# Encoder layer on one core: buffers for z, two later stores of weight sums, and the first token loads requested by ScalarE

## The chip, the cores and the metric

The kernel runs on one core of a Trainium2 chip. The metric is the device time of one execution in microseconds, as a median of several runs.

## The reference

One encoder layer is applied to two sequences of 1024-wide tokens, a prompt of 256 and a sample of 2048. The six parts of the input projection are called q, k, v, z_a, u and z_f here, each 512 wide.

```
h = rms_norm(x, g_pre);  proj = h @ w_in          # q, k, v, z_a, u_f, z_f
y_a = neighbourhood_attention(q, k, v, rpb)       # window of 8 rows x 16 columns on a grid 64 wide
y_f = real(fft2(u_f over tokens and 64 features)) @ w_fourier + b_fourier
mixed = [rms_norm(y_a) * silu(z_a), rms_norm(y_f) * silu(z_f)]
out = x + rms_norm(mixed @ w_out, g_post)
```

All data are float32.

## The kernel before

**Products in three passes.** A float32 product is made from operands split into a rounded part h (written by ScalarE as a cast) and a rest l (written by VectorE as source minus h). `mm3` (L163) then issues three matmuls, h by h, h by l and l by h. So each operand of TensorE costs one ScalarE instruction and one VectorE instruction before it can be used.

**Who orders the work.** From L602 to L971 the order on ScalarE, VectorE, GpSimd and SyncE is the order in which the program's lines run, and TensorE's order is by hand everywhere. Each engine takes its instructions strictly in that order. SyncE issues every DMA of the kernel; a DMA that has to wait for its data or its buffer holds up all those behind it in SyncE's order. Buffers come from pools with tags, and an instruction that takes a buffer waits until the last reader of that buffer, often a store, is through.

**Stage 1 (L623 to L754), first tokens.** v and u are made for six tiles c of 128 tokens, two of the prompt and four of the sample. For the first three tiles the loads come in four parts kp of the contraction, each with two k of v's weights (`RV`) and two of each token tile (`x_part`, L617). `split_w` scales a weight by gpre on ScalarE (L258) and VectorE (L259), `x_split` splits tokens (L288, L289). v's twelve groups come first on TensorE, then u's, whose weights `fold_u` has to form on GpSimd (L269). Before all this TensorE runs idle matmuls (L229), and ScalarE loads its function table and warms it up (L604, L605). `r_sum` forms sums of v's and u's weights, and `r_put` (L456) stores them to `sD`, 1 MB each: five stores, number 0 at L675 and numbers 1 to 4 at L724 to L726, two for c = 3 and two for c = 4. They are read again from L467 on. `iv_get` (L323) loads the reciprocal norms of the sample's tokens spread over all partitions, `n_load` (L389) loads a quarter of transposed sample tokens, 1 MB, `n_scale` (L400) multiplies them by gpre and the reciprocal norm on VectorE, `n_sum` combines them, and `n_first` (L429) splits one of the results: a ScalarE cast of 128 by 2048 (L432) and a VectorE subtraction of the same size (L433).

**Stage 2 (L757 to L792), the prompt's other products.** Sixteen blocks b of z_f, z_a, k and q for the 256 prompt tokens, each with 24 matmuls of 256 columns. `wz_load` (L698) loads the weights of one block, 512 KB; `b_raw` (L562) splits them (L566 and L567, or L569 and L570 for q). It works two blocks ahead: block b carries `b_raw(b + 2)`, then one of `n_scale` (two instructions), `n_sum` or nothing, then perhaps `n_first` or `op_split`. At the end of each block ScalarE evacuates the product (L788) into a buffer of the tag f, of which there are 3, and SyncE stores it (L790, L792). The results of stage 1 leave through the same three buffers (`vu_out`, L335).

**Stage 3 (L819 to L848) and stage 4 (L834 to L969).** v and u of the rest, and then z_f, z_a, k and q of the sample, are made by a scheme with fewer products: sixteen rounds i with seven products j, from sums of weights (`w_sums`, L534, split in `a_split`, L545) and sums of tokens. Within a round VectorE adds products up in tiles of the tag e (6 buffers of 512 floats; `e_`, L853: u0, u2, u4, u3) and writes two outputs o of 1024 floats each, in the tag f (3 buffers), which are stored at j = 5 and j = 6 (L878, L880).

**The Fourier stage inside rounds 8 to 15.** For 16 values n2, `u_load` (L364) fetches a slice of u, `u_split` (L369) splits it (ScalarE L371, VectorE L372), and `u_stage1` (L374) multiplies it by a 128-point transform (`pz`), copies the result z out of the accumulator on ScalarE (L379) and stores it to `ZD` (L380). Each round takes three of them, at j = 1, 3 and 5. z has the tag f, whose other two buffers hold the round's outputs. ScalarE's copy of z stands in order before its casts for the next weights (L550) and for the next slice (L371).

**After L971** the four DMA and vector engines are ordered by a planner; the change touches nothing there.

Of the kernel before, what the change touches and what calls it, by code (L numbers as in the profile page):

```python
# [10 lines left out]
F32 = mybir.dt.float32  # L11
# [151 lines left out]
def mm3(nc, out, lh, ll, rh, rl, first, last):  # L163
    nc.tensor.matmul(out, lh, rh, start=first, stop=False)  # L164
    nc.tensor.matmul(out, lh, rl, start=False, stop=False)  # L165
    nc.tensor.matmul(out, ll, rh, start=False, stop=last)  # L166


def build(tc, A, O):
    nc = tc.nc  # L170
# [24 lines left out]
    ones = cst.tile([128, 1], F32, name="ones")  # L195
# [17 lines left out]
    st = ph.enter_context(tc.tile_pool(name="st", bufs=2))  # L213
# [17 lines left out]
    def gt(shape, dtype, name):  # L231
        return gp.tile(shape, dtype, tag="g", name=name)

    def load(shape, src, name):
        t = gt(shape, F32, name)
        nc.sync.dma_start(t, src)
        return t
# [7 lines left out]
    def k8(dtype, name, shape=(128, 4, 512)):  # L245
        return hp.tile(list(shape), dtype, tag="k8", name=name, bufs=NK)
# [27 lines left out]
    def xsrc(c):  # L274
        return A["xt"][c] if c < 2 else A["xs"][c - 2]
# [47 lines left out]
    def iv_get(c0, n):  # L323
        t = ivb[c0] = hp.tile([128, 1024], F32, tag="vw", name="iv", bufs=3)
        nc.sync.dma_start(t[:, :128 * n],
                          ivD[c0:c0 + n].rearrange("(o c) p -> o (c p)", o=1).to_broadcast([128, 128 * n]))
# [47 lines left out]
    def u_stage1(n2):  # L374
        t = uu_.pop(n2)
        pz = ps.tile([128, 512], F32, tag="b", name="pz", bufs=2)
        mm3(nc, pz, f1h, f1l, t[:, 0], t[:, 1], True, True)
        z = st.tile([128, 512], F32, tag="f", name="z", bufs=3)
        nc.scalar.copy(z, pz)  # L379
        nc.sync.dma_start(ZD[:, n2, :], z)  # L380

# [7 lines left out]
    def n_load(x):  # L389
        if type(x) is tuple:  # L390
            nq[x] = k8(F32, "nx")
            nc.sync.dma_start(nq[x], A["xq"][0, x[0], x[1]])
            return
        nx = [k8(F32, "nx") for kh in range(2)]
        for kh in range(2):
            for b in range(2):
                nq[x, kh, b] = nx[kh][:, 2 * b:2 * b + 2]
                nc.sync.dma_start(nq[x, kh, b], A["xq"][1, kh, b][:, 2 * x:2 * x + 2])

    def n_scale(x, kh, b, ks=range(4)):  # L400
        v_ = nq[kh, b] if x is None else nq[x, kh, b]
        for k in ks if x is None else range(2):
            kk = 4 * kh + 2 * (x or 0) + k
            nc.vector.scalar_tensor_tensor(out=v_[:, k], in0=v_[:, k], scalar=gpre[:, kk:kk + 1],
                                           in1=ivb[2 if x is None else 10][:, 512 * b:512 * b + 512], op0=ALU.mult, op1=ALU.mult)
# [23 lines left out]
    def n_first(j):  # L429
        src = nq[((0, 0), (1, 0), (0, 0), (0, 1), "t3", (1, 0), (1, 1))[j]]  # L430
        h, l = bnew[0, j] = [k8(F32R, "x" + x) for x in "hl"]
        nc.scalar.copy(h, src)  # L432
        nc.vector.tensor_tensor(out=l, in0=src, in1=f_(h), op=ALU.subtract)  # L433
# [22 lines left out]
    def r_put(x):  # L456
        nc.sync.dma_start(sD[x], (RU[1], RV[0], RU[0], RU[1], RV[1])[x])
# [26 lines left out]
    def et(name):  # L484
        return st.tile([128, 512], F32, tag="e", name=name, bufs=6)
# [76 lines left out]
    def b_raw(b):  # L562
        wh, wl = [gt(BS, F32R, "w" + x) for x in "hl"]
        src = wp_[b]
        if b < 12:
            nc.scalar.copy(wh, src)  # L566
            nc.vector.tensor_tensor(out=wl, in0=src, in1=wh.bitcast(F32), op=ALU.subtract)  # L567
        else:
            nc.scalar.activation(wh, src, AF.Copy, scale=-0.125)  # L569
            nc.vector.scalar_tensor_tensor(out=wl, in0=src, scalar=-0.125, in1=wh.bitcast(F32), op0=ALU.mult,  # L570
                                           op1=ALU.subtract)
        wb[b] = wh, wl
# [28 lines left out]
    man = ExitStack()  # L601
    man.enter_context(tc.manual_schedule(engines=MAN))  # L602
    warm = cst.tile([128, 1], F32, name="warm")
    nc.scalar.preload_act_table_set("natural_log_exp_and_others")  # L604
    nc.scalar.copy(warm, ones)  # L605
    f1 = st.tile([128, 128], F32, name="f1", bufs=1)
    f1h = st.tile([128, 128], F32R, name="f1h", bufs=1)
    f1l = st.tile([128, 128], F32R, name="f1l", bufs=1)
# [1 line left out]
    acc, xs, xh, xm = {}, {}, {}, {}  # L610
# [6 lines left out]
    def x_part(c, kp):  # L617
        if kp == 0:
            xs[c] = gt(BS, F32, "xr")
        ks = slice(2 * kp, 2 * kp + 2)  # L620
        nc.sync.dma_start(xs[c][:, ks], xsrc(c)[:, ks])

    nc.sync.dma_start(RV[0][:, 0], A["wv"][0][:, 0])  # L623
    nc.sync.dma_start(gpre, A["gpre"])
# [1 line left out]
    x_part(1, 0)  # L626
    nc.sync.dma_start(RV[0][:, 1], A["wv"][0][:, 1])
    x_part(2, 0)
    for kp in range(4):
        ks = slice(2 * kp, 2 * kp + 2)  # L630
        v = part(RV[kp // 2], kp)
        if kp:
            nc.sync.dma_start(v, part(A["wv"][kp // 2], kp))
            for c in range(3):
                x_part(c, kp)
        split_w("v", v[:, 0:1], (0,))
        x_split(0, ks)
        if kp == 0:
            x_split(1, ks)
        split_w("v", v[:, 1:2], (0,))  # L640
        if kp:
            x_split(1, ks)
        x_split(2, ks)
# [54 lines left out]
    def wz_load(n):  # L698
        for x in range(n):
            wp_.append(load(BS, A["wz"][len(wp_)], "wr"))  # L700
# [17 lines left out]
    for c in range(3, 6):  # L718
        if c == 3:
            iv_get(0, 2)  # L720
        if c < 5:
            wz_load(3)
            x_split(c + 1)
        if c < 5:  # L724
            for x in range(2 * c - 5, 2 * c - 3):
                r_put(x)  # L726
        if c == 4:
            n_load((0, 0))
            iv_get(2, 8)
            xp = k8(F32, "xp", (128, KC, 256))  # L730
            hp_, lp_ = [k8(F32R, "p" + x, (128, KC, 256)) for x in "hl"]
            for k in range(KC):
                for t in range(2):
                    ts = slice(128 * t, 128 * t + 128)
                    nc.vector.scalar_tensor_tensor(out=xp[:, k, ts], in0=xs[t][:, k], scalar=gpre[:, k:k + 1],
                                                   in1=ivb[0][:, ts], op0=ALU.mult, op1=ALU.mult)
            nc.scalar.copy(hp_, xp)
            nc.vector.tensor_tensor(out=lp_, in0=xp, in1=f_(hp_), op=ALU.subtract)
        if c == 5:
            n_load((1, 0))  # L740
            b_raw(0)
            b_raw(1)
        p_mm("v", c, range(4))
        vu_out("v", c)
        if c == 5:
            for b in range(2, 4):
                b_raw(b)
                n_scale(None, 0, 0, range(2 * b - 4, 2 * b - 2))
        p_mm("u", c, range(4))
        if c == 3:  # L750
            iv_rows(2, 8)
        vu_out("u", c)
        if c == 3:
            iv_put(2, 8)  # L754


    for b in range(16):  # L757
        kind, blk = divmod(b, 4)
        if b < 10:
            wz_load(1)  # L760
        if b in (0, 2):
            n_load((b // 2, 1))
        if b == 10:
            op_load(0)
        if b == 12:
            op_load(1)
        if 2 <= b < 14:
            b_raw(b + 2)
        if 2 <= b < 8:
            x, y = divmod(b, 2)  # L770
            n_scale(None, *divmod(x, 2)[::-1], range(2 * y, 2 * y + 2))
        elif 8 <= b < 12:
            n_sum(b - 8)
        if b in (3, 5, 12, 13):
            n_first((3, 5, 12, 13).index(b))
        if b > 13:
            op_split(b - 14)
        p = mmt(512)[:, :TP]
        wh, wl = wb.pop(b)
        for k in range(KC):  # L780
            mm3(nc, p, wh[:, k], wl[:, k], hp_[:, k], lp_[:, k], k == 0, k == KC - 1)
        o = st.tile([128, 256], F32, tag="f", name="f", bufs=3)
        if kind % 2:
            i, d = p, o
        else:
            i = p.rearrange("p (b r c) -> p b r c", b=2, c=32)
            d = o.rearrange("p (r b c) -> p b r c", b=2, c=32)
        nc.scalar.activation(d, i, AF.Silu if kind < 2 else AF.Copy)  # L788
        if kind < 2:
            nc.sync.dma_start(zD[kind, blk * 128:blk * 128 + 128, :TP], o)  # L790
        else:
            nc.sync.dma_start((kD if kind == 2 else qD)[blk, :, :TP], o)  # L792
# [41 lines left out]
    for i in range(16):  # L834
# [48 lines left out]
        for j in range(7):  # L883
# [29 lines left out]
            if sg == 0:  # L913
                x, y = divmod(7 * (pr - 1) + j, 14)
# [17 lines left out]
            for f, d in ((u_load, 0), (u_split, 4), (u_stage1, 6)):  # L932
                x = 7 * pr + j - 7 - d
# [43 lines left out]
    kp = es.enter_context(tc.tile_pool(name="kp", bufs=2, side="right"))  # L977
# [569 lines left out]
    for k in range(2, len(G) + 1):  # L1547
        pr, i = divmod(k, 9)
        g, f = G[k] if k < len(G) else None, G[k - 1] if k else None
# [19 lines left out]
        x = k // 2 + 1  # L1569
# [63 lines left out]
        if 32 <= k < 36:  # L1633
            x, d = k - 32, atiles[k - 32]
# [122 lines left out]
```

## Time and profile before

| what | value |
|---|---|
| median of 3 runs | 982.48 us (980.37 to 988.38) |
| the profiled execution | 981.93 us, span 980.1 us |
| TensorE busy | 963.9 us (98%) |
| VectorE, ScalarE, GpSimd busy | 705.7, 497.3, 431.0 us |
| granted TensorE clock | 0.999 |
| DMA, mean over the span | 286 GB/s |

In the profile's rows PE is TensorE, DVE VectorE, ACT ScalarE, POOL GpSimd and SPq the DMA issues of SyncE. A row of the timeline gives start, duration, engine, line, operation, output and input, how many were merged, and in brackets the idle time ahead of it and what ended that. A row of groups gives busy time and mean nanoseconds, then the idle time ahead of the group. A row of windows gives the length of the stretch, the busy time and count of each engine, the granted clock, the share of the DMA engines and the GB/s. Matmuls overlap, so the pace of TensorE is the distance from start to start.

### The profile page before, as it was taken

The page shows a single profiled execution, that of the slowest core. Times are in us where ns is not written, and L with a number is a line of the kernel's source. Part 1 is how long each engine was busy: PE and PEld are TensorE (multiplying, and loading weights), DVE is VectorE, ACT ScalarE, POOL GpSimd, SP SyncE. Part 2 cuts the span into 40 slices and gives each one's busy share as a digit, 9 for nine tenths or more (in the row PEclk, how much of TensorE's full clock was granted, in tenths as well). Part 3 has the DMA queues.
Part 4 walks back from the last instruction along what each step waited for, and adds up shares of the span by engine and source line. Part 5 has one row for each costly group of instructions (what it writes and reads, how often), then busy time and mean ns, then how long its engine had stood idle before and what let it go on. Part 6 is the DMA issues. An engine that isn't in the chain of part 4 may idle for free.

```text
span 980.1 us, 17001 instructions
## 1 busy us (share of the span) xinstructions
PE 963.9 (98%) x5761; PEld 804.7 (82%) x5761; DVE 705.7 (72%) x1301; ACT 497.3 (51%) x1068; POOL 431.0 (44%) x400
## 2 busy tenths in 40 slices
PE   9999999999999999999999999999999999999996
PEld 7889988888888888887887879888888888888885
DVE  5747988687886877796776445776666666659997
ACT  5836676423335533333334255677666676654443
POOL 3200002455752202755664033477587686534544
PEclk9999999999999999999999999999999999999999
DMA  8899586557759996598887998598787998979993
GB/s 311 321 375 375 195 319 247 196 197 275 275 200 361 360 411 231 214 368 287 316 310 266 332 334 324 184 297 277 243 239 233 290 317 260 294 250 335 332 347 123
DMA packets 146450, 279.89 MB, mean 286 GB/s; under 512 B 13162, under 2 KB 84284, under 8 KB 142972
## 3 DMA queue, kind: packets, MB, share of 16 engines
q1 hardware_dynamic: 146364, 278.80, 81.7%
q8 instruction: 46, 0.75, 0.3%
q14 instruction: 40, 0.33, 0.1%
HBM read 184.37 MB, written 101.72 MB: 292 GB/s over the span
## 4 chain that ended last, share of the span: by engine, by line
PE 52%; DVE 1%; DMA 1%; issue 1%; POOL 1%; ACT 0%; DVEq 0%; SPq 0%; POOLq 0%; ACTq 0%
PE po L1427 20%; PE pv L1497 5%; PE ptb L1481 5%; PE s L1176 4%; PE mm L166 3%; PE mm L165 3%; PE mm L164 3%; PE pab L1019 2%; DMA ZD<-z 1%; PE py L164 1%; PE py L166 1%; PE py L165 1%; PE pz L165 0%; DVE ut L372 0%; PE ppq L1057 0%
## 5 line engine op out<-in xcount | busy, mean ns | idle before, releaser
L164 PE MATMUL mm<-xh,wa 128*128 128x512 f32 x448 | 174.4, 389 | 0.0
L166 PE MATMUL mm<-xh,wa 128*128 128x512 f32 x448 | 174.4, 389 | 0.0
L165 PE MATMUL mm<-xl,wa 128*128 128x512 f32 x448 | 174.4, 389 | 0.0
L536 POOL TENSOR_TENSOR ws<-wr 128x512 f32<-128x512 f32 x16 | 23.2, 1449 | 229.7 <-DMA wr<-wz 217.6
L1210 POOL TENSOR_SCALAR w<-w,m 128x480 f32<-128x480 f32 (+6 forms) x136 | 85.9, 644 | 43.7 <-DVE m L1207 38.5
L165 PEld LDWEIGHTS mm<-xl,wa 128*128 128x128 f32 x448 | 84.1, 188 | 17.6
L164 PEld LDWEIGHTS mm<-xh,wa 128*128 128x128 f32 x448 | 84.1, 188 | 17.6
L166 PEld LDWEIGHTS mm<-xh,wa 128*128 128x128 f32 x448 | 84.1, 188 | 17.4
L1427 PE MATMUL po<-wo,yh 128*128 128x512 f32 x272 | 90.5, 413 | 0.0
L551 DVE TENSOR_TENSOR wa<-wr,wa 128x512 fp32r<-128x512 f32 x60 | 67.0, 1125 | 32.2 <-ACT wa L550 32.1
L1203 ACT ACTIVATE w<-w,m 128x480 f32<-128x480 f32 (+6 forms) x136 | 79.2, 585 | 15.4 <-DVE m L1198 15.4
L1427 PE MATMUL po<-w,yh 128*128 128x512 f32 x280 | 86.7, 391 | 0.0
L1198 DVE CUSTOM_DVE_ANT_1 w<-s,tb 128x360 f32<-128x360 f32 (+5 forms) x124 | 62.5, 541 | 8.4 <-PE s L1176 7.6
L589 POOL TENSOR_TENSOR mt<-mt,rmask 128x880 f32<-128x880 f32 (+2 forms) x24 | 51.6, 2165 | 38.3 <-DVE mt L585 30.2
L165 PE MATMUL mm<-vl,xh 128*128 128x512 f32 x168 | 65.5, 390 | 0.2 <-DVE vl L482 0.2
L164 PE MATMUL mm<-vh,xh 128*128 128x512 f32 x168 | 65.4, 389 | 0.0
L166 PE MATMUL mm<-vh,xl 128*128 128x512 f32 x168 | 65.4, 389 | 0.0
L872 DVE TENSOR_TENSOR f<-u,mm 128x512 f32<-128x512 f32 x64 | 43.5, 680 | 26.0 <-PE mm L166 21.0
L1427 PEld LDWEIGHTS po<-w,yh 128*128 128x128 f32 x280 | 52.3, 188 | 10.8 <-issue 0.2
L1481 PE MATMUL ptb<-ident,w 128*120 128x128 f32 (+5 forms) x428 | 59.6, 277 | 0.1
L1497 PEld LDWEIGHTS pv<-pt,v 120*64 120x64 f32 (+6 forms) x896 | 48.2, 136 | 12.9 <-issue 11.4
L1485 DVE COPY pt<-ptb 120x384 f32<-120x384 f32 (+6 forms) x72 | 41.0, 569 | 24.6 <-PE ptb L1481 24.0
(253 smaller groups left out, 2391.8 us busy)
## 6 DMA issues: line engine op xcount, KB each, us to landing
wr<-wz SPq DMA_DIRECT2D x48, 512.0 KB
vl<-sD SPq DMA_DIRECT2D x20, 512.0 KB
xm<-xm SPq DMA_DIRECT2D x9, 1024.0 KB
oD<-ofs SPq DMA_DIRECT2D x18, 512.0 KB
of<-oD SPq DMA_DIRECT2D x18, 512.0 KB
yr<-yD SPq DMA_DIRECT2D x34, 256.0 KB
zD<-f SPq DMA_DIRECT2D x16, 512.0 KB
woD<-wo SPq DMA_DIRECT2D x16, 512.0 KB
```

The source lines that it names most:

```text
L164: nc.tensor.matmul(out, lh, rh, start=first, stop=False)
L165: nc.tensor.matmul(out, lh, rl, start=False, stop=False)
L166: nc.tensor.matmul(out, ll, rh, start=False, stop=last)
L551: nc.vector.tensor_tensor(out=o[:, 1], in0=src, in1=o[:, 0].bitcast(F32), op=ALU.subtract)
L589: nc.gpsimd.tensor_tensor(out=o, in0=i, in1=rmask[:, m0:m0 + n].unsqueeze(2).to_broadcast([128, n, 80]), op=ALU.add)
L872: nc.vector.tensor_tensor(out=dst(f, b), in0=src(uu[u]), in1=src(p), op=op)
L1198: nc.vector.tensor_tensor_reduce(out=rows(g["w"][b][:, h, :n], w), in0=rows(g["s"][2 * b + h][:, :n], w), in1=tv, scale=1.0, scalar=3.0e38 ...
L1203: nc.scalar.activation(w, w, AF.Exp, bias=m[:, h:h + 1], scale=-1.0, accum_out=m[:, 2 + h:3 + h])
L1210: nc.gpsimd.tensor_scalar(w, w, m[:, 4 + h:5 + h], 1.0, ALU.mult, ALU.mult)
L1427: nc.tensor.matmul(p, (d["l"] if x == 2 else d["h"])[:, c], w(n, int(x == 1), c), start=j == 0, stop=j == 11)
L1481: nc.tensor.transpose(ptb[h][:nk, j * 128:j * 128 + 128], g["w"][b][:, h, c0:c0 + nk], ident)
L1497: nc.tensor.matmul(p[hs, b], g["v"][:nk, v, hs], g["pt"][b][:nk, h, j * 128:j * 128 + 128], start=j == 0, stop=j == len(ch) - 1)
```

## The change

z takes a buffer of the tag e in place of the tag f. The first parts (kp = 0) of the three token tiles are requested by ScalarE in place of SyncE, and ScalarE's table load and warm-up stand behind these requests. Of the stores of weight sums, number 1 stays at c = 3, number 2 goes to c = 4 behind `n_load((0, 0))` and `iv_get(2, 8)`, and numbers 3 and 4 go into blocks 5 and 7 of the prompt's products. At c = 5, the two `b_raw` stand ahead of the four `n_scale`, and behind them `n_first(0)`, which was in block 3; the weight load of block 0 and `n_load((0, 1))` come there too, ahead of the store of u for c = 5.

```
-        z = st.tile([128, 512], F32, tag="f", name="z", bufs=3)
+        z = et("z")
         nc.scalar.copy(z, pz)
         nc.sync.dma_start(ZD[:, n2, :], z)
...
-    nc.scalar.preload_act_table_set("natural_log_exp_and_others")
-    nc.scalar.copy(warm, ones)
...
-        nc.sync.dma_start(xs[c][:, ks], xsrc(c)[:, ks])
+        (nc.sync if kp else nc.scalar).dma_start(xs[c][:, ks], xsrc(c)[:, ks])
...
     x_part(2, 0)
+    nc.scalar.preload_act_table_set("natural_log_exp_and_others")
+    nc.scalar.copy(warm, ones)
...
-        if c < 5:
-            for x in range(2 * c - 5, 2 * c - 3):
-                r_put(x)
+        if c == 3:
+            r_put(1)
         if c == 4:
             n_load((0, 0))
             iv_get(2, 8)
+            r_put(2)
...
         if c == 5:
-            for b in range(2, 4):
-                b_raw(b)
-                n_scale(None, 0, 0, range(2 * b - 4, 2 * b - 2))
+            b_raw(2)
+            b_raw(3)
+            wz_load(1)
+            n_load((0, 1))
+            n_scale(None, 0, 0)
+            n_first(0)
...
-        if b < 10:
+        if 1 <= b < 10:
             wz_load(1)
-        if b in (0, 2):
-            n_load((b // 2, 1))
+        if b == 2:
+            n_load((1, 1))
+        if b in (5, 7):
+            r_put(b // 2 + 1)
...
-        if b in (3, 5, 12, 13):
-            n_first((3, 5, 12, 13).index(b))
+        if b in (5, 12, 13):
+            n_first((5, 12, 13).index(b) + 1)
```

## Prediction

> **What bounds the kernel now.** I read the engine shares first, then the waits of TensorE, then every distance from start to start of its matmuls in stages 1 to 4.
>
> ```profile
> PE 963.9 (98%) x5761; PEld 804.7 (82%) x5761; DVE 705.7 (72%) x1301; ACT 497.3 (51%) x1068; POOL 431.0 (44%) x400
> ```
> ```profile
> PE pz L165 <- DVE ut L372: 3.6, 3, 2.0
> PE mm L166 <- DVE wl L567: 2.0, 2, 1.1
> ```
>
> TensorE is the bound, and no edit removes a matmul. The change can only win back time in which TensorE stands or runs slowly. That is 980.1 - 963.9 = 16 us over the whole span, and the two longest waits above lie where the change works. Three places matter: the Fourier slices, the prompt's blocks, and the first microseconds.
>
> **z in the sums' buffers.** The first row of the next fence is the group of z copies in the rounds 8 to 15; then come two of them, the store ahead of the first, and what TensorE did.
>
> ```profile
> L379 ACT COPY z<-pz 128x512 f32<-128x512 f32 x16 | 9.4, 587 | 48.6 <-DMA ZD<-z 34.9 <-PE pz L166 8.6 <-DVE u L950 3.6
> ```
> ```profile
> 440.84 0.33 SPq L380 DMA_DIRECT2D ZD<-z  x1
> ```
> ```profile
> 450.52 0.59 ACT L379 COPY z<-pz 128x512 f32<-128x512 f32 x1 [8.47 <-DMA ZD<-z]
> ...
> 516.42 0.59 ACT L379 COPY z<-pz 128x512 f32<-128x512 f32 x1 [8.73 <-DMA ZD<-z]
> ```
> ```profile
> 455.13 0.50 PE L165 MATMUL pz<-ut,f1h 128*128 128x512 f32 x1 [1.95 <-DVE ut L372]
> 455.47 0.40 PE L166 MATMUL pz<-ut,f1l 128*128 128x512 f32 x1
> 455.70 0.39 PE L164 MATMUL mm<-xh,wa 128*128 128x512 f32 x1
> ...
> 519.04 0.51 PE L164 MATMUL pz<-ut,f1h 128*128 128x512 f32 x1 [0.45 <-ACT ut L371]
> 520.97 0.50 PE L165 MATMUL pz<-ut,f1h 128*128 128x512 f32 x1 [1.42 <-DVE ut L372]
> ```
>
> The two outputs hold two of the three f buffers, so each z waits for the store of the z before it: issued at 440.84, it frees the copy at 450.52, 9.7 us later. In that time ScalarE cannot make the casts queued behind the copy, for the next weights and the next slice. VectorE's subtractions follow late, and TensorE waits 1.95 us at 455.13 and 0.45 + 1.42 us behind the copy of 516.42. That is 3.82 us. The first matmuls after a wait also come slower, 0.34 us apart (455.13 to 455.47) against 0.23 (455.47 to 455.70). The five slow starts at these places add some 0.7 us. Lost in all: 4.5 us. With three or more free e buffers no z waits for a store, the casts run on time, and all 4.5 us come back. Removing the other waits in the 34.9 us is worth nothing, because TensorE did not stand there. The slice's loads and the round's stores behind z on SyncE's queue only move earlier. What now waits for z's store is a sum of the next round. A round asks for seven e buffers (four sums, three z) out of six, so a buffer comes round again after six requests, nearly a whole round. A round takes 7 products of 12 matmuls and three slices of 3, 93 matmuls at 0.227 us or 21 us, against a store of 9.7 us. Ends: 4.5 us gained, and a loss if reuse comes at once (the third rival). I take 4.5.
>
> **The prompt's blocks.** Rows of TensorE, then groups of VectorE in 83 to 123.3 us, then windows.
>
> ```profile
> 73.06 0.28 PE L164 MATMUL mm<-ph,wh 128*128 128x256 f32 x1
> 73.18 0.28 PE L165 MATMUL mm<-pl,wh 128*128 128x256 f32 x1
> ...
> 91.67 0.39 PE L166 MATMUL mm<-ph,wl 128*128 128x256 f32 x1 [0.94 <-DVE wl L567]
> ...
> 98.79 0.39 PE L166 MATMUL mm<-ph,wl 128*128 128x256 f32 x1 [1.10 <-DVE wl L567]
> ...
> 123.14 0.39 PE L164 MATMUL mm<-vh,xh 128*128 128x512 f32 x1
> ```
> ```profile
> L567 DVE TENSOR_TENSOR wl<-wr,wh 128x1024 fp32r<-128x1024 f32 x8 | 9.8, 1222 | 2.3 <-ACT wh L566 2.3
> L433 DVE TENSOR_TENSOR xl<-nx,xh 128x2048 fp32r<-128x2048 f32 x4 | 9.2, 2289 | 0.0
> ```
> ```profile
> 58.00:78.00 20.00, 20.00 (x110) 17.39 (x109) 7.42 (x9) 8.02 (x9) 0.00 (x0) 1.00 1.02 415
> 83.00:100.00 17.00, 14.96 (x123) 14.55 (x122) 16.73 (x18) 11.66 (x15) 0.00 (x0) 1.00 1.00 396
> 100.00:123.30 23.30, 22.69 (x184) 21.96 (x182) 23.30 (x17) 14.68 (x18) 0.00 (x0) 1.00 0.54 177
> ```
>
> 384 matmuls at 0.12 us would take 46.1 us. They take 123.14 - 73.06 = 50.1 us, so 4.0 us are lost, and another 0.5 us at the first product behind them, where the start after next is again late. VectorE is the cause: busy in all of 83 to 123.3 us but for 2.3 us at its beginning. From 83.27 on the stage ends when VectorE's list ends. `n_first(0)` takes its subtraction, 2.29 us (2.2 net of overlap), out of that list and puts it where VectorE is busy 7.42 us of 20. Its ScalarE cast goes the same way, and the two subtractions and four scalings of c = 5 only change order. So the list ends 2.2 us sooner.
>
> What may undo it is how the list begins:
>
> ```profile
> 77.73 0.69 ACT L339 ACTIVATE uo<-mm,invt 128x512 f32<-128x512 f32 x1 [3.42 <-DMA vN<-vo]
> ...
> 82.19 1.04 ACT L566 CAST wh<-wr 128x1024 fp32r<-128x1024 f32 x1
> ```
> ```profile
> 73.09 1.23 DVE L567 TENSOR_TENSOR wl<-wr,wh 128x1024 fp32r<-128x1024 f32 x1 [5.38 <-issue]
> 77.09 1.42 DVE L404 SCALAR_TENSOR_TENSOR nx<-nx,gpre,iv 128x512 f32<-128x512 f32 x2 [2.77 <-DMA iv<-ivD]
> ...
> 83.27 1.23 DVE L567 TENSOR_TENSOR wl<-wr,wh 128x1024 fp32r<-128x1024 f32 x1 [2.30 <-ACT wh L566]
> ```
> ```profile
> 60.59 0.33 SPq L457 DMA_DIRECT2D sD<-ru  x1
> 63.04 0.33 SPq L457 DMA_DIRECT2D sD<-rv  x1
> ...
> 64.22 0.32 SPq L325 DMA_DIRECT2D iv<-ivD  x1
> ```
>
> ScalarE's cast for block 4 comes at 82.19, in order behind the evacuation of u at 77.73, which waited for a store. The reciprocal norms, requested at 64.22, land at 77.09, 12.9 us later, with the DMA engines full (1.02, 415 GB/s). The stores at 60.59 and 63.04 and number 2 no longer stand ahead of them: 3 MB less, some 7 us at 415 GB/s, so they land near 70 us. The scalings then follow the two splits: 73.09 plus 2 x 1.2 plus 2 x 1.42 us (each row holds two) is 78.3. The cast of `n_first(0)`, twice the size of the one of 1.04 us at 82.19, ends near 80.3 and its subtraction near 82.6. ScalarE evacuates u only behind the cast, near 80 instead of 77.73. The f buffers it needs after that wait for stores that now have 3 MB less ahead of them, so I expect the cast for block 4 within 0.5 us of 82.2. If the buffer that holds the split back to 73.09 comes sooner, all of this is 2 to 3 us earlier, and the whole 4.5 us could return. `wz_load` and `n_load((0, 1))` at c = 5 are issued in the time in which SyncE waits for u's evacuation anyway. The two stores in blocks 5 and 7 cost 2 x 1 MB at 396 GB/s, 2.6 us each, ahead of weight loads and of the stores that free the f buffers. Weights are used four blocks (11.5 us) after their request, and after 100 us the DMA engines are half idle (0.54). Ends: 0 and 4.5 us gained. I take 2.2, the one subtraction.
>
> **The first microseconds.**
>
> ```profile
> 0.73 1.28 ACT L604 ACT_TABLE_LOAD   x1 [0.73 <-PEq L1748]
> 2.03 0.19 ACT L605 COPY warm<-ones 128x1 f32<-128x1 f32 x1
> 4.17 0.72 ACT L258 ACTIVATE wc<-rv,gpre 128x512 fp32r<-128x512 f32 x1 [1.95 <-DMA gpre<-gpre]
> ...
> 9.77 0.72 ACT L258 ACTIVATE wc<-rv,gpre 128x512 fp32r<-128x512 f32 x1 [2.54 <-DMA rv<-wv]
> ```
> ```profile
> 1.64 0.91 SPq L621 DMA_DIRECT2D xr<-xt  x2
> ```
> ```profile
> 10.84 0.49 PE L164 MATMUL mm<-wc,xh 128*128 128x512 f32 x1 [0.39 <-ACT xh L288]
> ```
> ```profile
> 2.00:9.00 7.00, 6.71 (x30) 5.27 (x30) 2.51 (x5) 2.73 (x7) 0.00 (x0) 1.00 0.82 238
> ```
> ```profile
> 5.24 0.50 PE L164 MATMUL mm<-wc,xh 128*128 128x512 f32 x1
> ...
> 23.80 0.39 PE L164 MATMUL mm<-wc,xh 128*128 128x512 f32 x1
> ```
>
> v's 72 matmuls for three tiles run from 5.24 to 23.80, 18.6 us against 72 x 0.227 = 16.3, so 2.2 us are lost. Two token requests cost SyncE 0.91 us, three cost 1.4 us. Without them every later request goes out up to 1.4 us sooner, among them v's weights that ScalarE got at 9.77. ScalarE starts with three requests, 1.4 us by SyncE's rate, then 1.28 + 0.19 us: done near 3.6, while gpre lands at 4.17. So the moved table load costs nothing; without that cover of 0.6 us it would cost what goes beyond it, and at twice SyncE's rate per request that is 0.8 us. The DMA engines were 0.82 busy in 2 to 9 us, so 1.26 us of transfer time can be filled. Ends: 0.8 lost and 2.2 gained; I take half of the 1.26, or 0.7 gained.
>
> By the Trainium skill, "DMA: Bandwidth & Descriptors", section "Issuing engines are not separate DMA queues", requests from two engines share the same 16 DMA engines and save only the time of issuing; the share of 0.82 above leaves room for that saving, and by the rule alone at full DMA engines the term would be 0 (976 to 975 in the sum). By its page "ScalarE: Activation LUTs", section "What ACT_TABLE_LOAD costs", 1.38 us of drain follow a load of 1.28 us, which would make ScalarE late by some 0.8 us; here the warm-up at 2.03 directly follows a load that ends at 2.01, so the trace does not bear it out.
>
> **The sum.** 981.93 - 4.5 - 2.2 - 0.7 = 974.5 us. The profiled execution is 0.55 us under the median of the three runs, 982.48, so it stands for them.
>
> **The rivals.**
>
> All stalls go: the chain of stores eases so much that the prompt's blocks run at 0.12 us throughout. For it speaks that iv, u's evacuation and the f buffers all wait for one full DMA queue; against it, that VectorE needs about 3.3 us a block from block 8 on (a split of 1.2 and `n_sum` or `n_first` of 2.29, less overlaps) against 2.88 on TensorE. 981.93 - 4.5 - 4.5 - 2.2 = 970.7.
>
> The prompt's gain is given back: ScalarE's cast of `n_first(0)` pushes u's evacuation and all behind it, or the two stores delay the f buffers, so that VectorE's list starts or stands 2.2 us later. For it speaks that the cast at 82.19 has only 1.1 us to spare; against it, the 3 MB. 981.93 - 4.5 - 0.7 = 976.7.
>
> The z stores hold up the sums, the slower side: if a sum is given the buffer of the last z at once, it waits up to 9.7 us per round for the store, on ScalarE or VectorE. In the rounds VectorE is free for 116 - 80.2 us (row below), about 6.5 us a round; what exceeds that, 3.2 us in six rounds, adds 19 us, and 2.9 us are gained elsewhere: 998. It decides only once the buffer is asked for less than 9.7 us after the store, and the rotation of six speaks against that.
>
> ```profile
> 430.00:546.00 116.00, 111.98 (x489) 91.30 (x489) 80.19 (x94) 45.11 (x77) 62.24 (x35) 1.00 0.87 309
> ```
>
> The change does not do what it says for z: the slices wait for their own loads or for VectorE instead, and the 4.5 us stay. 981.93 - 2.9 = 979.0.
>
> **How the numbers follow.** Forecast 974.5 (within 1.5 us): 0.45. All stalls go: 0.13. Prompt's gain lost: 0.21. z's gain replaced: 0.14. z holds the sums: 0.04. Something else slower: 0.03. From 970.0 to 980.5 lie the first four and their noise, 0.85 or so. A measurement of this kernel can tell about 1%, 9.8 us; only the first rival, and it in part, goes beyond that: faster 0.11, same 0.84, slower 0.05.
>
> **What would show it.** Right: no z copy waits for ZD; no TensorE wait near 455 and 520; the last prompt block ends 2 us sooner after its first; the subtraction of `n_first(0)` lies before 83 us; ScalarE's first weight still starts near 4.2. Wrong: waits of sums for ZD; the cast for block 4 later than 84; the waits at blocks 6 and 8 unchanged; v's first 72 matmuls not shorter.

## The result and the profile after

The changed kernel takes 972.22 us (median of 8 runs, 971.13 to 973.84), the kernel before beside it 981.42 us (8 runs, 978.64 to 988.38). The ratio is 0.990, with a 95% interval of 0.9874 to 0.9926: 9.2 us less, against a forecast of 974.5 and about as much as the 1% that the prediction called the limit of what can be told. The profiled execution after took 971.13 us, with a span of 969.3 us against 980.1; its granted clock is 0.997, before 0.999, so the clock did not give the gain.

From the page of the changed kernel, the engine shares; below it all that is left of TensorE's waits (engine, line, what was waited for: us in all, times, longest).

```profile
PE 960.3 (99%) x5761; PEld 805.3 (83%) x5761; DVE 709.3 (73%) x1301; ACT 496.7 (51%) x1068; POOL 430.2 (44%) x400
```
```profile
PE idle L229 <- POOL onesq L225: 1.0, 1, 1.0
PE mm L164 <- ACT xh L288: 0.9, 1, 0.9
PE mm L165 <- DVE vl L482: 0.2, 1, 0.2
```

The waits for `ut` and for `wl`, 3.6 and 2.0 us before, are gone. To see where the time came from, the prediction's landmarks are looked up again. TensorE's timeline after:

```profile
6.29 0.50 PE L164 MATMUL mm<-wc,xh 128*128 128x512 f32 x1 [0.87 <-ACT xh L288]
...
23.14 0.39 PE L164 MATMUL mm<-wc,xh 128*128 128x512 f32 x1
...
72.40 0.28 PE L164 MATMUL mm<-ph,wh 128*128 128x256 f32 x1
...
118.69 0.39 PE L164 MATMUL mm<-vh,xh 128*128 128x512 f32 x1
```

| TensorE, start in us | before | after | gained in this stretch |
|---|---|---|---|
| first product of u | 23.80 | 23.14 | 0.66 |
| first product of the prompt's blocks | 73.06 | 72.40 | 0.00 |
| first product behind the blocks | 123.14 | 118.69 | 3.79 |
| first Fourier slice (`pz`) | 431.18 | 426.73 | 0.00 |
| last Fourier slice | 542.42 | 532.61 | 5.36 |

These are 9.81 of the span's 10.8 us. The remaining 1.0 us lies in the stages after, which the change does not touch. All thirteen kernels of this document have the same code there and take 436.7 to 438.5 us for it, so it is not claimed for the change.

**The slices.** The group of z copies on ScalarE in 420 to 536 us (busy us, mean ns, then the idle time ahead of it), then TensorE's group of the products behind `ut`, and the window:

```profile
L379 ACT COPY z<-pz 128x512 f32<-128x512 f32 x16 | 9.4, 589 | 27.6 <-PE pz L166 23.0 <-issue 4.5
```
```profile
L165 PE MATMUL pz<-ut,f1h 128*128 128x512 f32 x16 | 6.2, 389 | 0.0
```
```profile
420.00:536.00 116.00, 116.00 (x513) 96.05 (x512) 85.00 (x99) 45.70 (x78) 67.60 (x37) 1.00 0.92 329
```

Before, 34.9 of 48.6 us of ScalarE's idle time ahead of z ended with a store of z. Those were 5 of the 16 copies. Now no such wait is left: z waits for its own product (the 4.5 us of "issue" are one copy, at 524.24, right behind the last matmul of its product at 523.77), and TensorE is busy in all of the 116 us.

**The prompt's blocks.** First VectorE, then ScalarE, then SyncE's issues, in the changed kernel:

```profile
68.82 2.54 DVE L567 TENSOR_TENSOR wl<-wr,wh 128x1024 fp32r<-128x1024 f32 x2 [3.03 <-ACT wh L566]
71.28 2.73 DVE L404 SCALAR_TENSOR_TENSOR nx<-nx,gpre,iv 128x512 f32<-128x512 f32 x4
75.98 2.29 DVE L433 TENSOR_TENSOR xl<-nx,xh 128x2048 fp32r<-128x2048 f32 x1 [1.97 <-ACT xh L432]
79.76 1.23 DVE L567 TENSOR_TENSOR wl<-wr,wh 128x1024 fp32r<-128x1024 f32 x1 [1.48 <-ACT wh L566]
```
```profile
74.05 1.90 ACT L432 CAST xh<-nx 128x2048 fp32r<-128x2048 f32 x1 [4.31 <-DVE nx L404]
75.86 0.68 ACT L339 ACTIVATE uo<-mm,invt 128x512 f32<-128x512 f32 x1
...
78.69 1.04 ACT L566 CAST wh<-wr 128x1024 fp32r<-128x1024 f32 x1
```
```profile
59.07 0.33 SPq L325 DMA_DIRECT2D iv<-ivD  x1
...
88.31 0.47 SPq L457 DMA_DIRECT2D sD<-ru  x1
...
94.03 0.46 SPq L457 DMA_DIRECT2D sD<-rv  x1
```
```profile
83.00:100.00 17.00, 17.00 (x144) 17.00 (x144) 16.34 (x18) 9.64 (x13) 0.00 (x0) 1.00 1.02 395
100.00:118.70 18.70, 18.70 (x157) 18.54 (x155) 18.70 (x12) 13.25 (x16) 0.00 (x0) 1.00 0.65 233
```

The reciprocal norms are requested 5 us sooner than before (59.07 against 64.22), and the scalings follow the splits without a wait. The subtraction of `n_first(0)` begins at 75.98. VectorE's list for block 4 starts at 79.76, 7.36 us behind the first product of the blocks, against 83.27 and 10.21 before. VectorE is still busy in nearly all of 83 to 118.7 us, and the two stores fall into a time of full DMA engines (1.02), but TensorE no longer waits: the blocks take 46.29 us, and 384 times 0.12 is 46.1.

**The first microseconds.** ScalarE in the changed kernel (ACTq are its DMA issues):

```profile
0.74 0.89 ACTq L619 DMA_DIRECT2D xr<-xt  x2
1.66 0.45 ACTq L619 DMA_DIRECT2D xr<-xs  x1
2.14 1.28 ACT L627 ACT_TABLE_LOAD   x1 [2.14 <-issue]
3.43 0.19 ACT L628 COPY warm<-ones 128x1 f32<-128x1 f32 x1
5.22 0.72 ACT L258 ACTIVATE wc<-rv,gpre 128x512 fp32r<-128x512 f32 x1 [1.60 <-DMA gpre<-gpre]
...
7.94 0.73 ACT L258 ACTIVATE wc<-rv,gpre 128x512 fp32r<-128x512 f32 x1 [0.29 <-DMA rv<-wv]
```

The first weight starts at 5.22, not near 4.2: gpre comes 1.05 us later. The second part of v's weights is split at 7.94 in place of 9.77. In this profile 0.66 us are left of it at u's first product.

### The profile page after: what moved, and what is told of

The parts are those of the page before. It is cut to its first block, busy times and chain, and to the rows that moved or that the text cites. A ratio compares the mean times of both kernels' runs of the same rounds, so it can differ in the third digit from the quotient of the medians.

```text
span 969.3 us, 17001 instructions
## 1 busy us (share of the span) xinstructions
PE 960.3 (99%) x5761; PEld 805.3 (83%) x5761; DVE 709.3 (73%) x1301; ACT 496.7 (51%) x1068; POOL 430.2 (44%) x400
## 4 chain that ended last, share of the span: by engine, by line
PE 97%; DVE 1%; POOL 1%; issue 0%; DMA 0%; ACT 0%; DVEq 0%; SPq 0%; POOLq 0%; ACTq 0%
PE po L1432 20%; PE mm L165 18%; PE mm L166 18%; PE mm L164 18%; PE pv L1502 5%; PE ptb L1486 5%; PE s L1181 4%; PE pab L1024 2%; PE py L164 1%; PE py L166 1%; PE py L165 1%; DMA gpre<-gpre 0%; PE ppq L1062 0%; PE pz L166 0%; PE pz L165 0%
## 5 line engine op out<-in xcount | busy, mean ns | idle before, releaser
L1432 PEld LDWEIGHTS po<-w,yh 128*128 128x128 f32 x280 | 52.3, 188 | 10.8 <-issue 0.2
L550 ACT CAST wa<-wr 128x512 fp32r<-128x512 f32 x60 | 36.4, 617 | 45.1 <-PE mm L166 18.8
```

The lines of the kernel that those rows point to most:

```text
L1432: nc.tensor.matmul(p, (d["l"] if x == 2 else d["h"])[:, c], w(n, int(x == 1), c), start=j == 0, stop=j == 11)
```

## The experiments

**Each part of the change alone or undone**, four kernels beside the kernel before (980.93 us).

`z_only` is the kernel before with one line changed.

```
-        z = st.tile([128, 512], F32, tag="f", name="z", bufs=3)
+        z = et("z")
```

> The kernel before with z in the sums' buffers and nothing else. If z's waits for its own store are what held TensorE in rounds 8 to 15, the stretch from the first to the last pz matmul shrinks from 111.2 us to about 105.9 (as in the changed kernel, 532.61 - 426.73), everything ahead of it stays, and the time is 5.4 us under the kernel before. If instead that stretch became dense because the rounds start 4.5 us sooner against the DMA queue, at least 2 us of the waits stay and the gain is 3 us or less.

Measured: 976.1 us, ratio 0.9951 (0.9936 to 0.9965). The first to the last slice take 431.44 to 537.29, 105.85 us against 111.24 before: 5.4 us, where nothing earlier has changed. ScalarE's group in 420 to 536 us (the sixteenth copy lies behind the window):

```profile
L379 ACT COPY z<-pz 128x512 f32<-128x512 f32 x15 | 8.8, 588 | 27.6 <-PE pz L166 23.0 <-issue 4.5
```

So the slices' gain comes from this line alone, and it is the same with the other edits as without them (105.88 and 105.85 us).

`stores_back` is the changed kernel with the weight sums' stores 1 to 4 back at c = 3 and c = 4.

```
-        if c == 3:
-            r_put(1)
+        if c < 5:
+            for x in range(2 * c - 5, 2 * c - 3):
+                r_put(x)
...
-            r_put(2)
...
-        if b in (5, 7):
-            r_put(b // 2 + 1)
```

> The changed kernel with the stores 1 to 4 of weight sums back at c = 3 and c = 4. Theory A (one subtraction less in VectorE's list gives 2.2 us, the lighter DMA queue the other 1.6): the prompt's blocks take 47.8 us from first to last matmul instead of 46.2, the time is 1.6 us above the changed kernel. Theory B (the lighter DMA queue gives all, since the list starts 3.5 us sooner by it): the norms land near 76 again, the cast of n_first(0) stands ahead of u's evacuation and pushes the cast for block 4 to 83 or later, the blocks take 49.5 us or more, 3.5 us or more above the changed kernel.

`first_back` is the changed kernel with `n_first(0)` back in block 3.

```
-            n_first(0)
...
-        if b in (5, 12, 13):
-            n_first((5, 12, 13).index(b) + 1)
+        if b in (3, 5, 12, 13):
+            n_first((3, 5, 12, 13).index(b))
```

> The changed kernel with n_first(0) back in block 3. Theory A: VectorE's list is 2.2 us longer, the blocks take 48.4 us, 2.2 us above the changed kernel. Theory B: the list starts 1 to 2 us sooner still, since u's evacuation no longer stands behind the cast, and the blocks stay within 1 us of 46.2.

Measured: 976.74 us (ratio 0.9953, 0.9939 to 0.9968) and 975.49 us (0.9948, 0.9929 to 0.9966). These medians may not be the price of the edit alone. Each of the two profiles has a wait of 1.2 to 1.3 us near 350 us, in a stage that the edit does not touch; three other kernels have 0.3 us there and the rest none, and whether the edits bring it about is not shown. In the profile with the stores back the first matmuls also ran at half pace (below), which puts u's first product at 24.62 us, 1.5 us later. So the blocks are read by themselves, from their own first product on. VectorE with the stores back, then ScalarE's cast for block 4 there, then VectorE with `n_first(0)` back:

```profile
73.92 2.48 DVE L567 TENSOR_TENSOR wl<-wr,wh 128x1024 fp32r<-128x1024 f32 x2 [6.57 <-issue]
76.66 2.74 DVE L404 SCALAR_TENSOR_TENSOR nx<-nx,gpre,iv 128x512 f32<-128x512 f32 x4 [0.26 <-DMA iv<-ivD]
81.36 2.29 DVE L433 TENSOR_TENSOR xl<-nx,xh 128x2048 fp32r<-128x2048 f32 x1 [1.97 <-ACT xh L432]
84.86 1.23 DVE L567 TENSOR_TENSOR wl<-wr,wh 128x1024 fp32r<-128x1024 f32 x1 [1.20 <-ACT wh L566]
```
```profile
83.78 1.05 ACT L566 CAST wh<-wr 128x1024 fp32r<-128x1024 f32 x1
```
```profile
79.94 1.23 DVE L567 TENSOR_TENSOR wl<-wr,wh 128x1024 fp32r<-128x1024 f32 x1 [5.74 <-ACT wh L566]
...
85.30 2.28 DVE L433 TENSOR_TENSOR xl<-nx,xh 128x2048 fp32r<-128x2048 f32 x1
```

| | blocks, us | VectorE's list begins, us after the first block |
|---|---|---|
| before | 50.08 | 10.21 |
| stores back | 48.6 | 10.97 |
| `n_first(0)` back | 47.65 | 7.35 |
| changed kernel | 46.29 | 7.36 |

With the stores back the blocks are 2.3 us longer, with `n_first(0)` back 1.4 us. Together they are 3.7 of the 3.8 us of the change. With the stores back the row at 73.92 starts behind 6.57 us in which VectorE waited for nothing that the profile names; with them moved it starts at 68.82 (69.01 with `n_first(0)` back). With `n_first(0)` back the list begins just as soon, but it is one subtraction of 2.28 us longer. Neither the theory that the subtraction alone does it nor the one that the stores alone do it holds: the list starts sooner because the stores were moved, and it is shorter because of `n_first(0)`.

**What held the split.** The row at 73.92 names only "issue". The rows beside it tell more. With the stores back, these are TensorE's last two matmuls for u, which read the two halves xh and xl of c = 5's tokens, and ScalarE's next cast:

```profile
73.44 0.39 PE L165 MATMUL mm<-wc,xh 128*128 128x512 f32 x1
73.66 0.39 PE L166 MATMUL mm<-wc,xl 128*128 128x512 f32 x1
```
```profile
74.09 1.05 ACT L566 CAST wh<-wr 128x1024 fp32r<-128x1024 f32 x1 [3.81 <-PE mm L166]
```

The last read of xh ends at 73.83, and VectorE begins the split's subtraction at 73.92; the last read of xl ends at 74.05, and ScalarE begins the cast at 74.09. The programs built from the kernels agree: in the kernel before, `z_only` and `stores_back`, these two writes are given the very buffers of xh and xl of c = 5 (13 buffers of one tag hold tokens and weights), and VectorE's has to wait for TensorE. In the changed kernel and in `first_back` they are given the buffers of the raw weights of blocks 0 and 1, whose splits end at 65.8 us in the changed kernel. So no store held the split. Moving the stores in the program changed which buffer the split gets when the program is built.

The stores also act while the kernel runs: with them back, the scalings behind the split still wait 0.26 us for the norms, until 76.66, so another buffer for the split would by itself hardly have let them begin sooner. In the changed kernel they begin at 71.28 and wait for neither. No run has the one without the other.

`gpre_first` is the changed kernel with gpre requested ahead of v's first weights.

```
+    nc.sync.dma_start(gpre, A["gpre"])
     nc.sync.dma_start(RV[0][:, 0], A["wv"][0][:, 0])
-    nc.sync.dma_start(gpre, A["gpre"])
```

> The changed kernel with gpre requested ahead of v's first weights on SyncE. If gpre came late in the changed kernel (5.22 instead of 4.17) because it stood behind 256 KB on its own queue, ScalarE's first weight comes near 4.2 again and the first product near 5.3 instead of 6.29, u's first product 0.5 to 1 us sooner. If it came late because the three token loads share the DMA engines with v's first weights, those weights become what ScalarE waits for, and the first product stays within 0.3 us of 6.29.

Measured: 975.01 us, 0.9940 (0.9919 to 0.9961), worse than both expectations. ScalarE's first weight, TensorE's first product, and the window of 8 to 10 us:

```profile
6.68 0.72 ACT L258 ACTIVATE wc<-rv,gpre 128x512 fp32r<-128x512 f32 x1 [3.05 <-DMA rv<-wv]
```
```profile
7.74 0.50 PE L164 MATMUL mm<-wc,xh 128*128 128x512 f32 x1 [2.49 <-ACT xh L288]
```
```profile
8.00:10.00 2.00, 2.00 (x5) 1.54 (x5) 2.00 (x6) 1.98 (x5) 0.00 (x0) 0.53 0.90 237
```

Now v's weights come last, later than gpre did, and behind the gap of 2.49 us TensorE was granted half the clock (0.53): u's first product is at 26.02. When gpre itself landed cannot be seen here. The order of these two requests only changes which of the two ScalarE waits for last.

**Who requests the first tokens**, in two more groups (the kernel before 982.67 and 983.56 us). `sync_requests` is the changed kernel with SyncE requesting the first parts again, `two_requests` the one in which ScalarE requests two of the three, `one_request` the one in which it requests the third alone, behind its table load in the program.

```
# sync_requests
+        nc.sync.dma_start(xs[c][:, ks], xsrc(c)[:, ks])
# two_requests
+        (nc.sync if kp or c == 2 else nc.scalar).dma_start(xs[c][:, ks], xsrc(c)[:, ks])
# one_request, x_part(2, 0) behind the warm-up
+        (nc.scalar if kp == 0 and c == 2 else nc.sync).dma_start(xs[c][:, ks], xsrc(c)[:, ks])
# each in place of
-        (nc.sync if kp else nc.scalar).dma_start(xs[c][:, ks], xsrc(c)[:, ks])
```

> The changed kernel with the first three token loads requested by SyncE again (the table load still behind where they stood). If these requests gave 0.7 us, ScalarE's first weight comes at 4.2 instead of 5.2, the first product at 5.25, but u's first product 0.6 to 0.9 us later than the 23.14 of the changed kernel, and the time is 0.7 us above it. If the loads were bound by the DMA engines and not by SyncE's issue time, u's first product comes within 0.2 us of 23.14 and the time is the same.

> The changed kernel with only the two prompt tiles requested by ScalarE; the sample's tile goes to SyncE behind v's second weight. If gpre lands late because 384 KB of tokens share the DMA engines with 256 KB of v's weights, a third of the tokens less brings ScalarE's first weight from 5.2 to about 4.8 and the first product to 5.9, and u's first product 0.2 to 0.4 us sooner. If the request itself on a second queue delays gpre, the first weight stays at 5.2.

> The changed kernel with the two prompt tiles requested by SyncE as before and only the sample's tile by ScalarE, behind its table load. If the early requests on a second queue are what delays gpre, the first weight is back at 4.2 and the first product at 5.25, v's later weights come about 0.45 us sooner than with all requests on SyncE, u's first product comes at 23.2 to 23.5, and no gap is left in which the clock could fall. The time is that of the changed kernel within 0.5 us.

ScalarE's first weight in each, in that order:

```profile
4.18 0.72 ACT L258 ACTIVATE wc<-rv,gpre 128x512 fp32r<-128x512 f32 x1 [1.96 <-DMA gpre<-gpre]
```
```profile
5.92 0.72 ACT L258 ACTIVATE wc<-rv,gpre 128x512 fp32r<-128x512 f32 x1 [2.79 <-DMA gpre<-gpre]
```
```profile
5.21 0.72 ACT L258 ACTIVATE wc<-rv,gpre 128x512 fp32r<-128x512 f32 x1 [2.99 <-DMA gpre<-gpre]
```

| | first weight | first product | u's first product | median us | ratio to before |
|---|---|---|---|---|---|
| SyncE requests all | 4.18 | 5.25 | 23.69 | 972.04 | 0.9899 (0.9877 to 0.9922) |
| ScalarE one | 5.21 | 6.27 | 24.46 | 973.11 | 0.9899 (0.9863 to 0.9934) |
| ScalarE two | 5.92 | 6.99 | 25.39 | 973.15 | 0.9907 (0.9889 to 0.9926) |
| ScalarE three (changed kernel) | 5.22 | 6.29 | 23.14 | 972.22 | 0.9900 (0.9874 to 0.9926) |

The runs of one and two requests came out later than expected: a single early request of ScalarE is enough to delay gpre by 1 us, and the bytes that ScalarE asks for don't order the delays (two requests, in one profile, are worse than three, which gave 5.22 to 5.55 in seven kernels). In both, the first matmuls also ran at half pace. `one_request` did not hold its request back as meant: it went out at 0.91 us, since only its place among ScalarE's rows was moved and ScalarE does not wait for its table load there. Without any such request gpre is back at 4.18, and u comes 0.55 us later than in the changed kernel; of that nothing is seen in the medians.

**The gap ahead of the first product.** `idle_13` runs 13 idle matmuls first in place of 10, `idle_5` five.

```
-    for x in range(10):
+    for x in range(13):     # idle_13;  range(5): idle_5
```

> The changed kernel with 13 idle matmuls of TensorE at its start instead of 10 (same result). In the changed kernel the first product comes 0.9 us after the idle ones end, and in two of the other runs the products behind such a gap of 0.9 and 2.5 us came 0.42 us apart instead of 0.23. Theory: TensorE left idle loses its clock; three more idle matmuls, 1.2 us by the 0.4 us of one, close the gap, the first product stays within 0.4 us of 6.3, the products behind it come 0.23 us apart in this run, and the median is up to 0.7 us below the changed kernel. Rival: the slow products have another cause (their operands come late one by one) and come as before in some runs; the median does not move.

> The changed kernel with 5 idle matmuls of TensorE at its start instead of 10 (same result), so that some 3 us lie between the idle ones and the first product. If such a gap costs TensorE its clock, the granted clock falls to about 0.5 for some 3 to 4 us behind the first product, its products come 0.42 us apart, and u's first product comes 1.3 to 2 us later than the 23.14 of the changed kernel. If the slow pace has another cause, the clock stays at 1.00 and u's first product within 0.4 us of 23.3.

Measured: 972.86 us, 0.9904 (0.9885 to 0.9923), for 13, and 974.01 us (one run) for 5. With 13 the gap only shrinks to 0.69 us and u's first product comes at 23.30: the expected gain over 23.14 is not seen, and 972.86 lies within the spread of the changed kernel. With 5 the gap is 3.01 us, and matmuls that were 0.23 us apart are 0.43 us apart:

```profile
6.51 0.80 PE L164 MATMUL mm<-wc,xh 128*128 128x512 f32 x1 [3.01 <-ACT xh L288]
...
8.02 0.63 PE L164 MATMUL mm<-wc,xh 128*128 128x512 f32 x1
8.45 0.63 PE L165 MATMUL mm<-wc,xh 128*128 128x512 f32 x1
```

They stay so until about 10.1 us, and u's first product is at 24.69, 1.55 us later. So half the pace for 3.5 us came as expected; the granted clock, expected near 0.5, stayed at 1.00 in every window of these us. `idle_5` has fewer idle matmuls as well as the longer gap, but `gpre_first`, with all ten and a gap of 2.49 us, came to the same pace. The changed kernel's profile has a gap of 0.87 us and the full pace behind it. That is not a rule for such gaps: `stores_back`, with the same start and 0.85 us, has the half pace.

**How many buffers z needs.** `z_own_one` gives z one buffer of its own; the sums keep theirs to themselves.

```
-        z = et("z")
+        z = st.tile([128, 512], F32, tag="zo", name="z", bufs=1)
```

> The changed kernel with one buffer of z's own instead of the sums' six; the outputs keep all three of theirs. If z's number of buffers is what counts, this is what z had before: z waits for its own last store, up to 9 us, the pz stretch grows from 105.9 to 110 us or more, and the time is 4 to 5.5 us above the changed kernel. If the gain was the outputs' third buffer, the stretch stays at 106 and the time is the same.

Measured: 978.56 us, 0.9954 (0.9935 to 0.9974); the slices take 427.04 to 540.95, 113.9 us, more than before the change. ScalarE's group of z copies, then TensorE:

```profile
L379 ACT COPY z<-pz 128x512 f32<-128x512 f32 x16 | 9.4, 587 | 56.4 <-DMA ZD<-z 54.9 <-issue 1.5
```
```profile
516.00 0.50 PE L164 MATMUL pz<-ut,f1h 128*128 128x512 f32 x1 [1.53 <-ACT ut L371]
517.93 0.68 PE L165 MATMUL pz<-ut,f1h 128*128 128x512 f32 x1 [1.42 <-DVE ut L372]
518.41 0.63 PE L166 MATMUL pz<-ut,f1l 128*128 128x512 f32 x1
```
```profile
518.00:520.00 2.00, 2.00 (x5) 1.62 (x6) 0.47 (x1) 1.49 (x3) 0.00 (x0) 0.52 0.91 311
```

The wait for z's store is back on ScalarE, ahead of 10 of the 16 copies where it was 5 before the change, and with it the same kind of waits of TensorE for `ut`. This shows the mechanism from the other side: what counts is that a store of z need not end before the next copy. It also shows that such waits can cost the clock: 0.52 granted behind two of them.

**The two loads at c = 5.** `loads_back` puts the weight load of block 0 and `n_load((0, 1))` back into block 0.

```
-            wz_load(1)
-            n_load((0, 1))
...
-        if 1 <= b < 10:
+        if b < 10:
...
-        if b == 2:
-            n_load((1, 1))
+        if b in (0, 2):
+            n_load((b // 2, 1))
```

> The changed kernel with the weight load of block 0 and n_load((0, 1)) back in blocks 0. If they only fill time in which SyncE waits anyway, the prompt's blocks still take 46.2 us and the time is that of the changed kernel. If their place ahead of u's store matters, VectorE's list starts 1 us or more later or sooner than 7.4 us behind the first block, and with a later start the blocks take 0.5 to 1 us more.

Measured: 972.13 us, 0.9891 (0.9837 to 0.9946); the blocks take 72.56 to 118.85, 46.3 us. The place of these loads shows neither cost nor gain.

## Why the prediction was right, and where it was not

The three places were right, two of the three sizes were low, and one of these for a reason that the prediction did not have. The sum, 974.5, was 2.3 us above the median; the profiled execution, which is 1.1 us faster than the median, lies 3.4 us below the sum, 0.9 of it in the slices, 1.6 in the blocks and nearly all the rest in the stages that the change does not touch. The median lies in the range, between the forecast and the first rival (970.7), whose prompt step nearly came true and whose startup step did not. At 1.0% the gain is what the prediction called "same" and gave 0.84.

- **z in the sums' buffers, 4.5 us: right, 5.4 measured.** What it said to look for came true: no z waits for its store, TensorE has no wait near 455 and 520, and no sum waits for a z store, so the slower rival is not seen. `z_only` and `z_own_one` show the cause from both sides. One reading was too strong: not each z waited for the store before it, but 5 of 16. The term is short by some 0.9 us: starts in excess of the pace in the profile before, summed at the places named, give 4.63 us, and the working left out the slow starts at 431.76 and 432.10 (0.46 us together) and at 497.78 (0.11). The last 0.2 us are not placed.
- **The prompt's blocks, 2.2 us: right for the subtraction, 3.8 measured.** The step that did not hold is "so I expect the cast for block 4 within 0.5 us of 82.2". It came at 78.69. The prediction had the list one subtraction shorter but beginning as late as before; the list also begins 2.9 us sooner, counted from the first block. The forecast chain was real: with the stores back the cast is at 83.78 and the subtraction of `n_first(0)` ends at 83.65, as worked out for 82.6. But in the changed kernel the split that stood at 73.09 begins at 68.82, so scalings, cast and subtraction end at 78.3. The prediction named this condition ("if the buffer that holds the split back to 73.09 comes sooner, all of this is 2 to 3 us earlier, and the whole 4.5 us could return") and gave it to a rival at 0.13. It came true, but not in the way meant: that buffer, the one that TensorE reads to the end of u's products, came no sooner; the split was given another. Nothing in the profile before tells that the change would give it another, so that the rival's step came out is in part luck. The norms, put near 70 us, were there by 71.28 at the latest, when the scalings begin without a wait for them. Against the rival's own doubt, VectorE is still busy without a pause from 88.4 us on, yet TensorE no longer waits for it, because its list starts 2.9 us sooner and has 2.3 us less to do.
- **The first microseconds, 0.7 us: the size came out by luck, one step was wrong.** "While gpre lands at 4.17" assumed that gpre would land as before. It landed 1.05 us later, so the table load (done at 3.43, warm-up to 3.62) was hidden by more than the 0.6 us given, while the first product came 1.05 us later and v's 72 matmuls took 16.85 us in place of 18.56. Between them 0.66 us stay in the profile, and 0.0 in the medians: `sync_requests` has 972.04 against 972.22. As a cause of the 9.2 us this term is not shown. The profiles suggest why: the five kernels with this start and 10 idle matmuls have u's first product at 23.14 to 23.45 in four cases, against 23.69 to 24.03 in the three with all requests on SyncE, but at 24.62 in `stores_back`, where the gap that the late gpre opens was followed by half pace. How often that happens is not shown. By the Trainium skill, "DMA: Bandwidth & Descriptors", section "Issuing engines are not separate DMA queues", only issue time is saved by a second engine; the medians agree with the term of 0 that the prediction drew from it for full DMA engines.
- **The stores in blocks 5 and 7** go out at 88.31 and 94.03, into DMA engines at 1.02, and cost TensorE nothing: the blocks run at their floor of 46.1 us within 0.2.

## What to carry to other kernels

A buffer tag that long-lived results share with short-lived ones is as small as what the long-lived ones leave over; here it left one at times, and a store of 9.7 us under load stood in order ahead of casts that had nothing to do with it. When instructions are moved in a program whose buffers rotate, a tile elsewhere can get another buffer, with another last reader to wait for; so check what the first instruction of the list that sets the end waits for, and not only how long the list is. And a request moved to a second engine to save issue time can delay a small load on the first queue by more than it saves, so the instruction that waits for the small load is looked at first.

## What the runs showed of the hardware

- **A second requester delays a small load.** gpre, requested at 1.16 to 1.18 us, lets the first weight start at 4.17 to 4.18 us in the three kernels in which ScalarE requests nothing, and at 5.21 to 5.92 us in the nine in which ScalarE requests one to three token parts and gpre stands second on SyncE. Sharing of the DMA engines alone would make three requests worse than two, which they are not (5.22 to 5.55 in seven kernels against 5.92 in one). The cause is left open.
- **TensorE at half pace.** Behind the gap ahead of the first product, matmuls were 0.42 to 0.43 us apart for some 3.5 us in `idle_5` (gap 3.01 us), `gpre_first` (2.49), `two_requests` (1.80), `stores_back` (0.85) and `one_request` (0.65), and at 0.23 in `idle_13` (0.69), the changed kernel (0.87), `z_own_one` (1.0), `loads_back` (1.34) and `first_back` (1.41). v's 72 matmuls then take 18.1 to 18.4 us in place of 16.8 to 17.0. So every gap from 1.8 us up did it, and of the seven shorter ones two did, whatever their length. The Trainium skill, "TensorE: Matmul & The Clock Gate", section "Part 1: The HAM clock gate (the "warmup" mystery)", gives the two paces as 426.7 and 215.7 ns for 512 columns, and the first agrees with the rows at 8.02 and 8.45, while the fast one is 227 ns here; it puts the fall to the slower one behind an idle window of about 3.4 us, while here all five gaps ahead of it were shorter, two of them 0.65 and 0.85 us, so the measurement goes beyond that rule. The clock column of the windows shows it in `gpre_first` (0.53) and `two_requests` (0.50) but not in `idle_5`, `stores_back` and `one_request`, where it stays at 1.00: the pace has to be read from start to start.
- **ScalarE issues a DMA as fast as SyncE:** 0.89 us for two and 0.45 for one at its beginning, against 0.91 for two by SyncE before.
